# Decoder trunk on one core: the order of the block products in the FFNs, their weight sums, and a second plain channel pair

## The chip, the cores and the metric

The kernel runs on one core of a Trainium2 chip. The metric is the device time of one execution in microseconds. TensorE (PE in the profile) multiplies, VectorE (DVE), ScalarE (ACT) and GpSimd (POOL) do the rest, and SyncE (SP) issues most of the loads. Each engine takes its instructions in the order in which they were queued.

## The reference

Two layers over 512 tokens of 1024 channels, float32. Around each mixer (a gated DeltaNet in layer 0, spatial gating in layer 1) stand two half-step SwiGLU FFNs, four in all, with a norm before and after each part:

```python
def swiglu(h, w_gate, w_up, w_down):
    return (jax.nn.silu(h @ w_gate) * (h @ w_up)) @ w_down
...
x = x + 0.5 * rmsnorm(swiglu(rmsnorm(x, ng[0]), w_gate, w_up, w_down), ng[1])
```

The FFN is 2816 wide: `w_gate` and `w_up` are 1024 x 2816, `w_down` is 2816 x 1024. The change is in the FFNs alone.

## The kernel before

**Numbers.** Every float32 operand is kept as a high and a low part. `split` makes them: ScalarE casts the high part (L108), VectorE subtracts it from the source for the low part (L110). A product is then three matmuls: high by high, high by low, low by high.

**An FFN.** The 2816 channels are worked through in 11 pairs of 128 (`fp`, 256 channels). For each pair the gate and the up projection are computed, and `m` is their product after the SiLU. Then `proj_out` multiplies all of `m` with `w_down` (L332), into eight PSUM banks `y`, two for each of four token blocks.

**The first pair** is plain (`ffn_first`): for each half of the tokens, gate and up, two times 128 channels, eight blocks of depth and three matmuls of 128x128 by 128x256, 192 matmuls in all.

**The other ten pairs** take seven block products instead of eight (`seven`, once for gate and once for up: a group). The 256 channels, the 1024 deep and the 512 tokens are halved; sums of blocks of the weights and of the activations are made beforehand, and a group is seven products of 12 matmuls each (L393), into three of the eight banks: `pa`, `pb`, `pc`. Bank `pa` takes four products one on top of the other; after the first three of them `keep` (L401) saves what it holds so far by a ScalarE copy, before the next product adds to it. The products, by the names that the change gives them: p1 (weights `a11`, bank pa, then keep), p5 (`s1`, pc), p6 (`s2`, pa, then keep), p2 (`a12`, pb), p7 (`s3`, pa, then keep), p4 (`a22`, pa), p3 (`s4`, pc). After p2, p7, p4 and p3 a `sink` (`gate` or `up`) adds a kept copy to a bank (L477, L486), applies the SiLU (L479, L481) or multiplies into `m` (L488, L490).

`seven` is a generator; `ffn` advances a group and the one before it (`late`) in turns, which gives the order p1, p4 of the group before, p5, p3 of the group before, p6, p2, p7.

**Weights.** A planner queue holds all loads in the order of their use, each with a cost (1 for a plain half-depth tile, 3 for a group); `wget` takes the next and loads ahead until the cost of what is ready is 3. `wload_seven` prepares a group: two loads on SP's queue (L161) into tiles `raw`, of which there are four; the sums `su` (tile `wsum`): `su[:, 0]` and `su[:, 2]` on GpSimd (L165, L166), `su[:, 1]` and `su[:, 3]` on VectorE (L170, L174); and the splits into `wa` (a11, a12), `ws` (s1 to s4, two tiles) and `wd` (a22). All of these and the activations share 21 slots of one pool. Plain tiles are loaded by `wload` (L114) and split into `w`.

**Order.** The start of the kernel (the first loads, norms and splits) is written by hand; the rest of each engine's queue is put in order by a list scheduler, at compile time, from the program's order and a cost model.

Of the kernel before, what the change touches and what calls it, by code (L numbers as in the profile page):

```python
# [7 lines left out]
F32 = mybir.dt.float32  # L8
# [3 lines left out]
ALU = mybir.AluOpType  # L12
# [4 lines left out]
P = 128  # L17
S = 512
D = 1024
NT = S // P  # L20
KT = D // P
F = 2816
NF = F // P
# [4 lines left out]
class Trunk:  # L28
# [126 lines left out]
    def wload_seven(self, w, c0, part, spot):  # L155

        nc = self.nc
        raw = []
        for j in range(2):
            r = self.wp.tile([P, 4, 256], F32, tag="raw", name=self.nm("raw"))  # L160
            nc.sync.dma_start(out=r, in_=w[j * 512:(j + 1) * 512, c0:c0 + 256].rearrange("(k p) f -> p k f", p=P))  # L161
            raw.append(r)
        a = [[raw[j][:, :, i * P:(i + 1) * P] for j in range(2)] for i in range(2)]
        su = self.big([P, 4, 4, P], F32, name="wsum")
        nc.gpsimd.tensor_tensor(out=su[:, 0], in0=a[1][0], in1=a[1][1], op=ALU.add)  # L165
        nc.gpsimd.tensor_tensor(out=su[:, 2], in0=a[0][0], in1=a[1][0], op=ALU.subtract)  # L166
        w1 = self.big([P, 2, 2, 4, P], F32R, name="wa")
        for j in range(2):
            self.split(a[0][j], w1[:, 0, j], w1[:, 1, j])
        nc.vector.tensor_tensor(out=su[:, 1], in0=su[:, 0], in1=a[0][0], op=ALU.subtract)  # L170
        sums = []
        for n in range(2):
            if n:
                nc.vector.tensor_tensor(out=su[:, 3], in0=a[0][1], in1=su[:, 1], op=ALU.subtract)  # L174
            ws = self.big([P, 2, 2, 4, P], F32R, name="ws")
            self.split(su[:, 2 * n:2 * n + 2], ws[:, 0], ws[:, 1])
            sums += [(ws[:, 0, i], ws[:, 1, i]) for i in range(2)]
        if part == 0:
            spot.append(self.big([P, 2, 2, 4, P], F32R, name="wd"))
        w22 = spot[0][:, part]  # L180
        self.split(a[1][1], w22[:, 0], w22[:, 1])
        return {"a11": (w1[:, 0, 0], w1[:, 1, 0]), "a12": (w1[:, 0, 1], w1[:, 1, 1]),
                "s1": sums[0], "s2": sums[1], "s3": sums[2], "s4": sums[3], "a22": (w22[:, 0], w22[:, 1])}
# [136 lines left out]
            nc.sync.dma_start(out=store[:, c], in_=xo[:, c])  # L320


    def proj_out(self, get, nk, ntail, on_token, groups=(range(NT),), ready=None, need=None):

        need = need or (lambda kt: None)
        y = [[self.bank("y") for _ in range(2)] for _ in range(NT)]

        def step(kt, t, wt, hfs=(0, 1)):
            m = get(kt, t)
            for a, b in ((0, 0), (0, 1), (1, 0)):  # L330
                for hf in hfs:
                    self.nc.tensor.matmul(y[t][hf], m[a], wt[b][:, hf * 512:(hf + 1) * 512],  # L332
                                          start=(kt == 0 and a == 0 and b == 0),
                                          stop=(kt == nk - 1 and a == 1))

        nhead = nk - ntail
        tail = None
        for n, group in enumerate(groups):
            if n == 0:
                head = []  # L340
                for kt in range(nhead):
                    if kt == max(0, nhead - 10):
                        on_token.prepare()
                    need(kt)
                    wt, = self.wget()
                    if len(groups) > 1:
                        head.append(wt)
                    for t in group:
                        step(kt, t, wt)
                    self.tick()  # L350
                need(nk - 1)
                tail = self.wget(ntail)
            else:
                if n == 1:
                    self.drain_until(ready)
                for kt in range(nhead):
                    for t in group:
                        step(kt, t, head[kt])
                    self.tick()
            for t in group:  # L360
                last = t == NT - 1
                for i, kt in enumerate(range(nhead, nk)):
                    step(kt, t, tail[i], (0,) if last else (0, 1))
                    if i == 1 and len(groups) == 1:
                        self.tick()
                if last:
                    for i, kt in enumerate(range(nhead, nk)):
                        step(kt, t, tail[i], (1,))
                on_token(t, y[t][0], y[t][1])
                self.tick()  # L370
# [11 lines left out]
        return (slice(0, 256), slice(256, 512)) if first else (slice(0, S),)  # L382


    def seven(self, wts, a, sink):

        nc = self.nc
        ba, bb, bc = (self.bank("p" + n)[:, :256] for n in "abc")

        def prod(out, w, t, first, last):  # L390
            for k in range(4):
                for m, (x, y) in enumerate(((0, 0), (0, 1), (1, 0))):
                    nc.tensor.matmul(out, wts[w][x][:, k], t[y][:, k], start=(first and k == 0 and m == 0),  # L393
                                     stop=(k == 3 and m == 2), skip_group_check=not first)
            self.unit += 1
            if self.unit % 2 == 0:
                self.tick()

        def keep():
            s = self.tp.tile([P, 256], F32, tag="keep", name=self.nm("keep"), bufs=4)  # L400
            nc.scalar.copy(out=s, in_=ba)  # L401
            return s

        prod(ba, "a11", self.block(a, 0, 0), True, True)
        u1 = keep()
        yield
        prod(bc, "s1", self.tsum(a, 0), True, True)
        yield
        prod(ba, "s2", self.tsum(a, 1), False, True)
        u2 = keep()  # L410
        prod(bb, "a12", self.block(a, 1, 0), True, True)
        sink(0, 0, bb, u1)
        prod(ba, "s3", self.tsum(a, 2), False, True)
        u3 = keep()
        sink(1, 1, bc, u3)
        yield
        prod(ba, "a22", self.tsum(a, 3), False, True)
        sink(1, 0, ba, None)
        yield
        prod(bc, "s4", self.block(a, 1, 1), False, True)  # L420
        sink(0, 1, bc, u2)


    def plan_ffn(self, wg, wu, wd):
        self.plan_pair(wg, 0)
        self.plan_pair(wu, 0)
        for fp in range(1, NF // 2):
            spot = []
            self.plan_seven(wg, fp * 256, 0, spot)
            self.plan_seven(wu, fp * 256, 1, spot)  # L430
        self.plan_out(wd, NF, 5)
# [22 lines left out]
            nc.scalar.activation(out=sg, in_=pg[f], func=AF.Silu)  # L454
            nc.vector.tensor_tensor(out=m[:, f], in0=sg, in1=pu[f], op=ALU.mult)

    def ffn(self, a, on_token):
        nc = self.nc
        V = nc.vector
        self.unit = 0  # L460
        ms = []
        late = None
        for fp in range(NF // 2):
            if fp % 2 == 0:
                m4 = self.big([P, 4, S], F32, name="m")
            m = m4[:, fp % 2 * 2:fp % 2 * 2 + 2]
            ms.append(m)
            if fp == 0:
                self.ffn_first(a, m)
                continue  # L470
            sg = [self.half([P, S], name="sg") for _ in range(2)]
# [17 lines left out]
                elif i == 1:  # L489
                    V.tensor_tensor(out=m[:, 1, c], in0=sg[1][:, c], in1=ps if add is None else us[1][:, c], op=ALU.mult)  # L490

            for sink in (gate, up):
                wts, = self.wget()
                steps = self.seven(wts, a, sink)
                next(steps)
                if late:
                    next(late)
                next(steps)
                if late:
                    next(late, None)  # L500
                next(steps)
                late = steps
        for _ in late:
            pass
        split = {}

        def need(kt):
# [6 lines left out]
            b = split[kt // 2]  # L514
            return (b[:, 0, kt % 2, t * P:(t + 1) * P], b[:, 1, kt % 2, t * P:(t + 1) * P])

        self.proj_out(get, NF, 5, on_token, need=need)


class DeltaNet:  # L520
# [737 lines left out]
def trunk_kernel(ctx: ExitStack, tc: tile.TileContext, x, norm_g, ffn_w_gate, ffn_w_up, ffn_w_down,  # L1258
                 dn_w_in, dn_conv_w, dn_a_log, dn_dt_bias, dn_norm_g, dn_w_out, sg_w_in, sg_b_in,
                 sg_ln_g, sg_ln_b, sg_w_s, sg_b_s, sg_w_out, out):  # L1260
    K = Trunk(ctx, tc)
    nc = tc.nc
# [5 lines left out]
    st = St()  # L1268
# [54 lines left out]
    ffns = [[(ffn_w_gate[l, i], ffn_w_up[l, i], ffn_w_down[l, i]) for i in range(2)] for l in range(2)]  # L1323
    dn = DeltaNet(K, dn_w_in[0], dn_conv_w[0], dn_a_log[0], dn_dt_bias[0], dn_norm_g[0], dn_w_out[0])
    sg = SpatialGate(K, sg_w_in[0], sg_b_in[0], sg_ln_g[0], sg_ln_b[0], sg_w_s[0], sg_b_s[0], sg_w_out[0])
    K.plan_ffn(*ffns[0][0])
    dn.plan()
    K.plan_ffn(*ffns[0][1])
    K.plan_ffn(*ffns[1][0])
# [6 lines left out]
    def start(t):  # L1336
        w = K.big([P, D], F32, name="bt")
        gen = K.pre_norm(st.x[t // 2][:, t % 2], g0[:, 0], st.a, t, w, 1)
        next(gen)
        return gen  # L1340
# [5 lines left out]
    with tc.manual_schedule(engines={ET.SP, ET.Activation, ET.DVE, ET.Pool}):  # L1346
# [3 lines left out]
        first = [start(0), start(1)]  # L1350
# [9 lines left out]
        rest = [start(2), start(3)]  # L1360
# [2 lines left out]
    for t in range(2, NT):  # L1363
        K.tasks.append([K.clock + t, rest[t - 2]])

    K.ffn(st.a, boundary(1, 0.5, False, quad=False))
    with tc.issue_after(started[0]), tc.issue_after(started[1]):
        K.spawn(dn.consts())
    dn.run(st.a, boundary(3, 1.0, False))
# [29 lines left out]
```

## Time and profile before

| | |
|---|---|
| median of 3 runs | 2089.93 us (2089.32 to 2090.73) |
| profiled execution | 2089.82 us, span 2088.1 us |
| PE busy | 2018.2 us (97%) |
| DVE busy | 1346.7 us (64%) |
| ACT busy | 923.0 us (44%) |
| POOL busy | 378.9 us (18%) |
| instructions | 32220 |

Matmuls are pipelined, one begins before the one ahead has ended, and their ends are modelled; where TensorE works without a break the distance between two starts is the cost of one. Idle time of an engine counts only where something behind it is late. L12 is line 12 of the kernel before; many lines are helpers', so work is told apart by its tile.

### The profile page before, as it was taken

What the parts mean: (1) busy time and instruction counts of PE and PEld (TensorE: products, weight loads), DVE (VectorE), ACT (ScalarE), POOL (GpSimd) and SP (SyncE); (2) the same over time, 40 slices, a digit from 0 to 9 for tenths busy, and PEclk for the clock granted to TensorE, in tenths of its full rate; (3) what the DMA queues carried; (4) which work ended last, traced back from release to release, by engine and by line L of the source; (5) the groups of instructions that cost most, each with busy time, mean ns of one, the idle gap of its engine ahead of it and who ended that gap; (6) DMA issues with size and microseconds to landing.
All of it is one profiled execution on the core that took longest, in us unless ns stands there. A gap on an engine that the chain in (4) does not pass through costs nothing.

```text
span 2088.1 us, 32220 instructions
## 1 busy us (share of the span) xinstructions
PE 2018.2 (97%) x13182; PEld 1833.0 (88%) x13182; DVE 1346.7 (64%) x1803; ACT 923.0 (44%) x1640; POOL 378.9 (18%) x358
## 2 busy tenths in 40 slices
PE   7999999999999999999999999999999999999998
PEld 6999988888888899998889999888888889999887
DVE  5888652677846687875358887526465529777632
ACT  5554441585434554544245454424223426454521
POOL 3333100111142232320023222001000013232000
PEclk9999999999999999999999999999999999999999
DMA  4333352235221433336322333633322613333421
GB/s 143 102 103 100 112 203 72 91 102 151 92 77 62 142 91 101 101 102 212 101 71 81 102 104 99 217 101 110 107 87 87 223 50 103 101 94 99 172 91 41
DMA packets 159622, 229.63 MB, mean 110 GB/s; under 512 B 18745, under 2 KB 130673, under 8 KB 157042
## 3 DMA queue, kind: packets, MB, share of 16 engines
q1 hardware_dynamic: 150146, 195.90, 30.3%
q10 hardware_dynamic: 9328, 31.68, 3.9%
q8 instruction: 103, 1.69, 0.3%
q14 instruction: 45, 0.37, 0.1%
HBM read 213.34 MB, written 14.21 MB: 109 GB/s over the span
## 4 chain that ended last, share of the span: by engine, by line
PE 75%; DVE 14%; ACT 5%; issue 3%; POOL 2%; DMA 1%; ACTq 0%; DVEq 0%; POOLq 0%; SPq 0%
PE y L332 28%; PE pa L393 14%; PE pc L393 7%; PE pb L393 3%; DVE ws L110 2%; DVE wsum L170 2%; PE ph L198 2%; PE ph L200 2%; PE ph L199 2%; DVE wa L110 2%; ACT ws L108 1%; PE pv L198 1%; PE pu L198 1%; PE pv L199 1%; PE pu L199 1%
## 5 line engine op out<-in xcount | busy, mean ns | idle before, releaser
L332 PE MATMUL y<-w,ms 128*128 128x512 f32 x1632 | 370.7, 389 | 0.0
L332 PEld LDWEIGHTS y<-w,ms 128*128 128x128 f32 x1632 | 306.1, 188 | 63.3
L393 PE MATMUL pa<-hsh,ws 128*128 128x256 f32 x1280 | 259.9, 286 | 26.4 <-ACT keep L401 26.4
L110 DVE TENSOR_TENSOR w<-raw,w 128x1024 fp32r<-128x1024 f32 x162 | 195.8, 1223 | 68.9 <-ACT w L108 68.4
L393 PEld LDWEIGHTS pa<-hsh,ws 128*128 128x128 f32 x1280 | 211.5, 192 | 31.2 <-ACT keep L401 31.1
L108 ACT CAST ws<-wsum 128x1024 fp32r<-128x1024 f32 x160 | 166.9, 1050 | 161.5 <-DVE wsum L170 93.3
L165 POOL TENSOR_TENSOR wsum<-raw,raw 128x512 f32<-128x512 f32 x80 | 126.9, 1586 | 576.9 <-PE pb L393 124.9
L110 DVE TENSOR_TENSOR ws<-wsum,ws 128x1024 fp32r<-128x1024 f32 x160 | 206.5, 1302 | 17.8 <-ACT ws L108 17.7
L108 ACT CAST w<-raw 128x1024 fp32r<-128x1024 f32 x163 | 167.2, 1051 | 102.7 <-PE y L332 49.4
L393 PE MATMUL pa<-hsl,ws 128*128 128x256 f32 x640 | 181.5, 284 | 0.0
L310 DVE TENSOR_TENSOR bt<-y,gain 128x512 f32<-128x512 f32 x48 | 32.9, 688 | 180.4 <-ACT junk L306 179.5
L401 ACT COPY keep<-pa 128x256 f32<-128x256 f32 x240 | 88.2, 367 | 124.1 <-PE pa L393 124.1
L393 PE MATMUL pa<-hsh,wd 128*128 128x256 f32 x640 | 129.9, 286 | 13.2 <-ACT keep L401 13.2
L206 POOL TENSOR_TENSOR rstd<-ss 128x1 f32<-128x1 f32 x24 | 8.0, 331 | 740.2 <-ACT junk L306 740.2
L166 POOL TENSOR_TENSOR wsum<-raw 128x512 f32<-128x512 f32 x80 | 132.0, 1650 | 0.1
L393 PE MATMUL pa<-hq,wa 128*128 128x256 f32 x960 | 128.7, 284 | 0.0
L393 PE MATMUL pc<-hsh,ws 128*128 128x256 f32 x640 | 128.2, 283 | 0.0
L393 PE MATMUL pc<-hq,ws 128*128 128x256 f32 x960 | 128.2, 283 | 0.0
L393 PE MATMUL pb<-hq,wa 128*128 128x256 f32 x960 | 128.1, 283 | 0.0
L393 PEld LDWEIGHTS pa<-hsl,ws 128*128 128x128 f32 x640 | 123.1, 192 | 0.0
L393 PEld LDWEIGHTS pa<-hq,wa 128*128 128x128 f32 x960 | 121.5, 193 | 0.0
L393 PEld LDWEIGHTS pb<-hq,wa 128*128 128x128 f32 x960 | 121.0, 192 | 0.0
(300 smaller groups left out, 4356.6 us busy)
## 6 DMA issues: line engine op xcount, KB each, us to landing
raw<-in_ffn_w_gate SPq DMA_DIRECT2D x88, 512.0 KB, 3.7
raw<-in_ffn_w_up SPq DMA_DIRECT2D x88, 512.0 KB, 4.5
raw<-in_ffn_w_down SPq DMA_DIRECT2D x88, 512.0 KB, 4.3
raw<-in_dn_w_in SPq DMA_DIRECT2D x32, 512.0 KB, 4.4
raw<-in_sg_w_in SPq DMA_DIRECT2D x32, 512.0 KB, 3.8
xs<-x ACTq DMA_DIRECT2D x20, 512.0 KB, 2.6
x<-xs ACTq DMA_DIRECT2D x10, 1024.0 KB, 10.8
raw<-in_sg_w_out SPq DMA_DIRECT2D x16, 512.0 KB, 4.3
```

What stands on the lines that cost most here:

```text
L108: self.nc.scalar.copy(out=hi, in_=src)
L110: e.tensor_tensor(out=lo, in0=src, in1=hi.bitcast(F32), op=ALU.subtract)
L165: nc.gpsimd.tensor_tensor(out=su[:, 0], in0=a[1][0], in1=a[1][1], op=ALU.add)
L166: nc.gpsimd.tensor_tensor(out=su[:, 2], in0=a[0][0], in1=a[1][0], op=ALU.subtract)
L170: nc.vector.tensor_tensor(out=su[:, 1], in0=su[:, 0], in1=a[0][0], op=ALU.subtract)
L198: nc.tensor.matmul(out, lhsT[0], rhs[0], start=start, stop=False)
L199: nc.tensor.matmul(out, lhsT[0], rhs[1], start=False, stop=False)
L200: nc.tensor.matmul(out, lhsT[1], rhs[0], start=False, stop=stop)
L310: nc.vector.tensor_tensor(out=tmp[:, c], in0=y, in1=grow[:, c], op=ALU.mult)
L332: self.nc.tensor.matmul(y[t][hf], m[a], wt[b][:, hf * 512:(hf + 1) * 512], start=(kt == 0 and a == 0 and b == 0), stop=(kt == nk - 1 and a ...
L393: nc.tensor.matmul(out, wts[w][x][:, k], t[y][:, k], start=(first and k == 0 and m == 0), stop=(k == 3 and m == 2), skip_group_check=not f ...
L401: nc.scalar.copy(out=s, in_=ba)
```

## The change

Three edits, in all four FFNs unless said otherwise.

1. `wload_seven`: `su[:, 0]` and `su[:, 2]` are computed on VectorE, not on GpSimd, and in the text they stand behind the splits of a11 and a12.
2. `seven` returns the seven products as steps with places (0, 1, 3, 4, 6, 9, 12). Group number n begins at place 7n, so the order becomes p1, p5, p4 of the group before, p6, p2, p3 of the group before, p7. The two steps left after the last group (its p4 and p3) are run by `proj_out`, one ahead of each of its first two token steps. The weights are taken (`wget`) and the banks allocated in the step that first uses them.
3. In the first FFN alone the second channel pair is plain too (`plain=2`).

```diff
@@ wload_seven
-        nc.gpsimd.tensor_tensor(out=su[:, 0], in0=a[1][0], in1=a[1][1], op=ALU.add)
-        nc.gpsimd.tensor_tensor(out=su[:, 2], in0=a[0][0], in1=a[1][0], op=ALU.subtract)
         w1 = self.big([P, 2, 2, 4, P], F32R, name="wa")
         for j in range(2):
             self.split(a[0][j], w1[:, 0, j], w1[:, 1, j])
-        nc.vector.tensor_tensor(out=su[:, 1], in0=su[:, 0], in1=a[0][0], op=ALU.subtract)
+        V = nc.vector
+        V.tensor_tensor(out=su[:, 0], in0=a[1][0], in1=a[1][1], op=ALU.add)
+        V.tensor_tensor(out=su[:, 1], in0=su[:, 0], in1=a[0][0], op=ALU.subtract)
         sums = []
         for n in range(2):
             if n:
-                nc.vector.tensor_tensor(out=su[:, 3], in0=a[0][1], in1=su[:, 1], op=ALU.subtract)
+                V.tensor_tensor(out=su[:, 2], in0=a[0][0], in1=a[1][0], op=ALU.subtract)
+                V.tensor_tensor(out=su[:, 3], in0=a[0][1], in1=su[:, 1], op=ALU.subtract)
@@ proj_out
                     for t in group:
+                        if rest:
+                            rest.pop(0)()
                         step(kt, t, wt)
@@ seven
+        def p1():
+            nonlocal ba
+            wts.update(self.wget()[0])
+            ba = self.bank("pa")[:, :256]
+            prod(ba, "a11", self.block(a, 0, 0), True)
+            keep(1)
+
+        def p5():
+            nonlocal bc
+            bc = self.bank("pc")[:, :256]
+            prod(bc, "s1", self.tsum(a, 0), True)
+
+        def p6():
+            prod(ba, "s2", self.tsum(a, 1), False)
+            keep(2)
+
+        def p2():
+            nonlocal bb
+            bb = self.bank("pb")[:, :256]
+            prod(bb, "a12", self.block(a, 1, 0), True)
+            sink(0, 0, bb, kept[1])
+
+        def p7():
+            prod(ba, "s3", self.tsum(a, 2), False)
+            keep(3)
+            sink(1, 1, bc, kept[3])
+
+        def p4():
+            prod(ba, "a22", self.tsum(a, 3), False)
+            sink(1, 0, ba, None)
+
+        def p3():
+            prod(bc, "s4", self.block(a, 1, 1), False)
+            sink(0, 1, bc, kept[2])
+
+        return {0: p1, 1: p5, 3: p6, 4: p2, 6: p7, 9: p4, 12: p3}
@@ plan_ffn
-        self.plan_pair(wg, 0)
-        self.plan_pair(wu, 0)
-        for fp in range(1, NF // 2):
+        for fp in range(plain):
+            self.plan_pair(wg, fp * 256)
+            self.plan_pair(wu, fp * 256)
+        for fp in range(plain, NF // 2):
@@ ffn
-            if fp == 0:
+            if fp < plain:
                 self.ffn_first(a, m)
                 continue
...
-            for sink in (gate, up):
-                wts, = self.wget()
-                steps = self.seven(wts, a, sink)
-                next(steps)
-                if late:
-                    next(late)
-                next(steps)
-                if late:
-                    next(late, None)
-                next(steps)
-                late = steps
-        for _ in late:
-            pass
+            for n, sink in enumerate((gate, up)):
+                first = (2 * (fp - plain) + n) * 7
+                for place, step in self.seven(a, sink).items():
+                    places[first + place] = step
+                for place in range(first, first + 7):
+                    if place in places:
+                        places.pop(place)()
+        rest = [places.pop(place) for place in sorted(places)]
...
-        self.proj_out(get, NF, 5, on_token, need=need)
+        self.proj_out(get, NF, 5, on_token, need=need, rest=rest)
@@ trunk_kernel
-    K.plan_ffn(*ffns[0][0])
+    K.plan_ffn(*ffns[0][0], plain=2)
...
-    K.ffn(st.a, boundary(1, 0.5, False, quad=False))
+    K.ffn(st.a, boundary(1, 0.5, False, quad=False), plain=2)
```

## Rows read from the trace of the kernel before

**Rows 1.** Page, part 1: engine, busy us, share of the span, instructions.

```profile
PE 2018.2 (97%) x13182; PEld 1833.0 (88%) x13182; DVE 1346.7 (64%) x1803; ACT 923.0 (44%) x1640; POOL 378.9 (18%) x358
```

**Rows 2.** Waits: engine, line, waited for, total us, times, longest us.

```profile
ACT ws L108 <- DVE wsum L170: 93.3, 55, 5.7
...
POOL wsum L165 <- DMA raw<-in_ffn_w_up: 59.0, 7, 11.2
...
PE pa L393 <- ACT keep L401: 39.6, 39, 2.1
```

**Rows 3.** Timeline of PE, 188 to 192 us: start, length, work, idle before.

```profile
188.36 0.28 PE L393 MATMUL pa<-hsh,ws 128*128 128x256 f32 x1
188.48 1.60 PE L393 MATMUL pa<-hq,wa 128*128 128x256 f32 x12
191.68 0.39 PE L393 MATMUL pa<-hsh,wd 128*128 128x256 f32 x1 [1.61 <-ACT keep L401]
191.91 0.28 PE L393 MATMUL pa<-hsl,wd 128*128 128x256 f32 x1
```

**Rows 4.** Timeline of ACT, 190 to 194 us.

```profile
190.31 1.04 ACT L108 CAST ws<-wsum 128x1024 fp32r<-128x1024 f32 x1 [4.08 <-DVE wsum L170]
191.27 0.37 ACT L401 COPY keep<-pa 128x256 f32<-128x256 f32 x1
...
193.32 0.36 ACT L401 COPY keep<-pa 128x256 f32<-128x256 f32 x1
```

**Rows 5.** Windows: stretch, busy us by engine, granted clock, DMA share, GB/s.

```profile
168.00:189.00 21.00, 21.00 (x178) 21.00 (x177) 14.19 (x19) 7.62 (x15) 5.58 (x4) 1.00 0.26 76
189.00:210.00 21.00, 18.41 (x152) 18.00 (x151) 20.02 (x26) 11.85 (x21) 6.10 (x4) 1.00 0.35 102
```

**Rows 6.** Groups of instructions: busy us, mean ns, idle before, releasers.

```profile
L110 DVE TENSOR_TENSOR ws<-wsum,ws 128x1024 fp32r<-128x1024 f32 x160 | 206.5, 1302 | 17.8 <-ACT ws L108 17.7
...
L165 POOL TENSOR_TENSOR wsum<-raw,raw 128x512 f32<-128x512 f32 x80 | 126.9, 1586 | 576.9 <-PE pb L393 124.9 <-DVE ws L110 116.9 <-PE pc L393 104.7
...
L170 DVE TENSOR_TENSOR wsum<-wsum,raw 128x512 f32<-128x512 f32 x80 | 84.1, 1052 | 13.9 <-POOL wsum L165 13.9
L110 DVE TENSOR_TENSOR wd<-raw,wd 128x512 fp32r<-128x512 f32 x80 | 83.3, 1054 | 2.8 <-ACT wd L108 2.8
...
L174 DVE TENSOR_TENSOR wsum<-raw,wsum 128x512 f32<-128x512 f32 x80 | 69.5, 869 | 1.1
```

**Rows 7.** Timeline of DVE, 110 to 116 us.

```profile
110.23 1.28 DVE L110 TENSOR_TENSOR wa<-raw,wa 128x512 fp32r<-128x512 f32 x2
111.44 0.68 DVE L170 TENSOR_TENSOR wsum<-wsum,raw 128x512 f32<-128x512 f32 x1
...
113.57 1.21 DVE L110 TENSOR_TENSOR ws<-wsum,ws 128x1024 fp32r<-128x1024 f32 x1
115.97 1.77 DVE L170 TENSOR_TENSOR wsum<-wsum,raw 128x512 f32<-128x512 f32 x1 [1.19 <-POOL wsum L165]
```

**Rows 8.** Timeline of POOL, 106 to 118 us.

```profile
115.90 1.29 POOL L166 TENSOR_TENSOR wsum<-raw 128x512 f32<-128x512 f32 x1
```

**Rows 9.** Timeline of ACT, 24 to 38 us.

```profile
31.44 1.05 ACT L108 CAST ws<-wsum 128x1024 fp32r<-128x1024 f32 x1 [5.75 <-DVE wsum L170]
...
35.85 2.04 ACT L108 CAST hq<-pt 128x512 fp32r<-128x512 f32 x4
```

**Rows 10.** Timeline of PE, 29 to 73 us.

```profile
29.33 1.04 PE L265 MATMUL pt<-ident,bt 128*128 128x128 f32 x8
...
32.95 0.28 PE L200 MATMUL pu<-hq,w 128*128 128x256 f32 x1
37.46 0.57 PE L198 MATMUL pg<-hq,w 128*128 128x256 f32 x2 [4.23 <-ACT hq L108]
...
71.90 1.60 PE L393 MATMUL pa<-hq,wa 128*128 128x256 f32 x12
```

**Rows 11.** Windows at the start of the second token half, columns as in rows 5.

```profile
39.00:45.00 6.00, 5.87 (x29) 5.87 (x30) 4.81 (x8) 2.15 (x3) 0.67 (x1) 0.54 0.23 77
```

More of the change, by code (lines that the diff above doesn't have):

```diff
@@ L320, in post_norm, with proj_out @@
             nc.sync.dma_start(out=store[:, c], in_=xo[:, c])
-    def proj_out(self, get, nk, ntail, on_token, groups=(range(NT),), ready=None, need=None):
+    def proj_out(self, get, nk, ntail, on_token, groups=(range(NT),), ready=None, need=None, rest=()):
         need = need or (lambda kt: None)
+        rest = list(rest)
         y = [[self.bank("y") for _ in range(2)] for _ in range(NT)]
@@ L382, in halves, with seven, prod @@
         return (slice(0, 256), slice(256, 512)) if first else (slice(0, S),)
-    def seven(self, wts, a, sink):
+    def seven(self, a, sink):
         nc = self.nc
-        ba, bb, bc = (self.bank("p" + n)[:, :256] for n in "abc")
-        def prod(out, w, t, first, last):
+        wts = {}
+        ba, bb, bc = None, None, None
+        kept = {}
+        def prod(out, w, t, first):
             for k in range(4):
@@ L397, in prod, with keep, plan_ffn @@
                 self.tick()
[L399 to L424, printed above, removed]
-        self.plan_pair(wg, 0)
-        self.plan_pair(wu, 0)
-        for fp in range(1, NF // 2):
+        def keep(n):
+            kept[n] = self.tp.tile([P, 256], F32, tag="keep", name=self.nm("keep"), bufs=4)
+            nc.scalar.copy(out=kept[n], in_=ba)
+        def p1():
[27 more added lines that the diff above has]
+        return {0: p1, 1: p5, 3: p6, 4: p2, 6: p7, 9: p4, 12: p3}
+    def plan_ffn(self, wg, wu, wd, plain=1):
+        for fp in range(plain):
+            self.plan_pair(wg, fp * 256)
+            self.plan_pair(wu, fp * 256)
+        for fp in range(plain, NF // 2):
             spot = []
@@ L455, in ffn_first, with ffn @@
             nc.vector.tensor_tensor(out=m[:, f], in0=sg, in1=pu[f], op=ALU.mult)
-    def ffn(self, a, on_token):
+    def ffn(self, a, on_token, plain=1):
         nc = self.nc
@@ L461, in ffn @@
         ms = []
-        late = None
+        places = {}
         for fp in range(NF // 2):
```

## The prediction

> **What bounds the kernel now.** I read the page first. TensorE is busy 2018.2 of 2088.1 us [rows 1], so all that any change can remove, short of matmuls, is about 70 us of idle TensorE. Who owns it is in the view of waits: one pair alone, a matmul into bank pa that waits for ScalarE's copy `keep`, accounts for 39.6 us in 39 stops [rows 2]. The reader is to see what it waits for: no weight, but the copy that saves bank pa before the next product accumulates into it.
>
> Then one stop, on TensorE's timeline. Twelve matmuls of a product take (1.60 - 0.28) / 11 = 0.12 us each, 1.44 us a product [rows 3]. At 188.48 p1 of a group is issued; p4 of the group before is next and could begin at 189.92, but begins at 191.68 and its second matmul comes 0.23 us after the first [rows 3]. The stop is shown as 1.61 us; it loses 191.68 - 189.92 + 0.11 = 1.87 us, so I add 0.26 to 0.27 to each stop shown. With that, the 39 stops lose 39.6 + 39 x 0.27 = 50.1 us. ScalarE's timeline says why: the copy ends at 191.64, behind a cast of weight sums that had waited 4.08 us for VectorE's L170 [rows 4]. ScalarE works in order, so a copy that takes 0.37 us is late by whatever cast stands ahead of it. VectorE is the late one: it is busy 20.02 of the 21 us from 189 on, and 14.19 in the 21 us before, in which TensorE never stops [rows 5]. So VectorE is full in clusters, though 64% busy over all [rows 1].
>
> **The change part by part.**
>
> *Order of the products.* Before, a group g and the one before it (') ran p1, p4', p5, p3', p6, p2, p7. After: p1, p5, p4', p6, p2, p3', p7. What stands between a product and the next one on the same bank: after p6 two products instead of one (p2, p3'), after p7 two instead of one (p1, p5 of the next group), after p1 two instead of three. Every stop seen so far is after p6 or p7, so each gets 1.44 us more cover. Work on TensorE is the same.
>
> How much of the stops goes? In the first FFN they are, in us: 1.16, 0.30, 0.39, 1.21; 1.05, 1.23; 0.54; 1.61, 0.99; 2.06; 0.52. I grouped them by the clusters in which VectorE is full, because a cluster that is behind stays behind: cover is spent once in it, not once a stop. So a cluster gives back its whole loss, but 1.44 us at most. The last stop (0.52, and one like it in each FFN) stays, for p4 still follows p7 at once at the tail. That gives, without the first FFN's first cluster, 5.1, 7.5, 7.5 and 7.3 us in the four FFNs: 27.4 us. Bounds: if every stop but the tail's goes, 50.1 - 4 x 0.79 = 47.0 us.
>
> Against it stands p1. A copy after p7 that ended 3.00 us after the modelled end of its product (188.64 to 191.64) cost 1.87, so a copy is free up to 1.12 us with one product behind it and up to 2.56 with two [rows 3, 4]. The copy after p1 at 188.48 (modelled end 190.08) ends at 193.68, 3.60 us late; three products covered it, two would not [rows 3, 4]. Pairing every copy with its product, I find 17 of 80 after p1 over 2.56 us, by 12.8 us in all. Between 0 (their casts come sooner, see next) and 12.8 I take half, 6.4 us.
>
> The sinks move with the products: each remains one VectorE or ScalarE instruction of 0.4 to 0.7 us, its banks are released at most two products later, and eight banks hold three of one group and two of the last. Cost nil; cover gone, a bank would have to be late by more than a group. The two leftover steps go in front of the first two token steps of the down projection, whose last bank is needed after two more: nil too.
>
> *Sums on VectorE.* L165 and L166 ran on GpSimd, 1.59 us on average for L165, and each of 80 weight sets has both [rows 6]. On VectorE no such sum with su[:, 0] stands, but L170 has the same shape and operand kinds: 0.68 us alone, and two instructions of that size in a row take 1.28, so the second adds 0.60 [rows 7]. 160 more instructions are 96 us. What is taken away: L170 began at 115.97 while GpSimd's L166 ran 115.90 to 117.19, and took 1.77 instead of 0.68 [rows 7, 8]. Means over the kernel against their value alone: L170 1.052, L174 0.869 and wd 1.054 against 0.68, ws 1.302 against 1.21 [rows 6, 7]. That is 80 x (0.37 + 0.19 + 0.37) + 160 x 0.09 = 89 us of VectorE time which GpSimd's presence costs. So 96 in, 89 out: nil on VectorE, and the chain sum, cast, difference is shorter by a GpSimd step. Bounds: 0 to 96 us taken back.
>
> The Trainium skill, SBUF — State Buffer, "Who interferes with whom", says that a VectorE instruction with two SBUF inputs contends with a GpSimd instruction that reads SBUF, and that one of them blocks. The trace agrees: 1.77 us against 0.68 for the same sum. By that rule the sums on VectorE would be paid for by the end of this blocking, as in my sum.
>
> In order, a first sum that waits for its raw tile now holds up VectorE: the sinks, the differences and through their casts the copies. On GpSimd it waited for raw data 59.0 us in seven cases for `up` alone [rows 2], harmlessly. Bounds: nil, or GpSimd's mean idle before it, 576.9 / 80 = 7.2 us a set [rows 6]. In the new text it stands behind the two splits of the same tiles, which need the data too, so I take nil.
>
> *Second plain pair.* One pair costs TensorE 192 matmuls instead of 168: 24 x 0.12 = +2.88 us. It takes the first seven-product set out of the start. There ScalarE idled 5.75 us for L170 before the cast at 31.44, and the four casts of the second token half stood behind it until 35.85 [rows 9]; TensorE had finished the first half at 33.07 and began the second at 37.46, after a stop of 4.23 us; from 39 to 45 us its granted clock was 0.54, about the lower of its levels (1.2 against 2.4 GHz) [rows 10, 11]. Without that: 33.07 + 96 x 0.12 + 192 x 0.12 = 67.6 us, where the third group then begins. It begins at 71.90 now [rows 10]: 4.3 us gained, with the extra matmuls paid. If the casts stay as late, the pair instead costs 2.88 less the 2.0 us of its own stops, +0.9. The transposes of the last token block end at 30.37 [rows 10] and four casts and differences need some 2 us, so I take the gain. Its four loads on SP's queue are the same bytes, one at a time instead of two. The first cluster's other stops, 0.39 and 1.21 (2.1 us lost), should go, as two weight sets fewer are prepared up to there.
>
> Sum: 27.4 + 4.3 + 2.1 - 6.4 = 27.4 us off. The profiled execution took 2089.82 (span 2088.1), the runs' median is 2089.93, the same within 0.01%. 2089.8 - 27.4 = **2062 us**.
>
> **Rivals.**
>
> 1. *The cover is only moved.* p1's shorter cover costs the full 12.8 us or more, because with earlier stops gone the copies are later still against TensorE. For it: after 188.48, p7's and p1's copies stand behind the same casts [rows 4]. Against it: those casts wait for L170, which gets faster. 12.8 instead of 6.4, and half of the start's gain: about 2071.
>
> 2. *All stops go.* If the end of the blocking also empties the clusters: 47.0 + 4.3, of which 2.0 are counted twice: about 2041.
>
> 3. *VectorE pays in full (slower).* In the stretches where it is full, 20 of 21 us, VectorE can take nothing more [rows 5]. Two sets there bring 4 x 0.60 = 2.4 us; four such stretches an FFN, 16 in all, 39 us, and the cover is used up: 2062 + 39 = 2101. It decides when more than 27.4 / 16 = 1.7 us of a stretch isn't paid by the blocking that ends. Against it: 89 us of stretched instructions lie mostly in just these stretches. The Trainium skill, Perfetto Trace Analysis, "Optimizing Scalar/DVE Operations", says that work of a saturated VectorE may be offloaded, even to GpSimd, which speaks against this move; it adds that the shared port can spoil that. The rows side with the second half.
>
> 4. *No change.* The order of ScalarE's queue is made anew from the new program; where its copies land behind other casts the stops come back at other places, and only the start's few us remain: 2086 to 2092.
>
> **How the numbers follow.** My forecast 0.50, rival 1 0.21, rival 2 0.10, rival 3 0.09, rival 4 0.10. About 0.2% (4 us) is what a measurement here tells from no change. Faster: the first three, and little of the fourth, 0.82; same 0.09; slower 0.09. The range reaches from near rival 2 past rival 1 to the edge of rival 4: 2044 to 2084.
>
> **What would show it.** Right: the waits of pa for `keep` fall under 15 us, TensorE's busy time rises by 2 to 3 us only, L170, L174 and wd show means near 0.68 us, VectorE's busy time stays within 25 us, the third group's weights start near 67.6. Wrong: stops before p6 (after p1) of over 12 us; VectorE idle before the first sum; stretches with VectorE at 21 of 21 and TensorE waiting for `ws` or `wa`.

## The result and the profile after

The changed kernel takes 2036.82 us (median; 2033.23 to 2039.26) against 2089.62 for the one before: ratio 0.975, 95% interval 0.9726 to 0.9774. It is faster, as forecast, but by 52.8 us where 27.4 were forecast, and outside the range of 2044 to 2084.

Parts of the page of the changed kernel (busy time), its view of waits, its groups of instructions, three of its windows of 21 us (columns as in [rows 5]) and rows of TensorE's timeline follow; three points mark rows left out. Line numbers have moved: the copy `keep` is L408, the products L400, the four sums L169, L170, L174, L175.

```profile
PE 2012.0 (99%) x13206; PEld 1833.3 (90%) x13206; DVE 1324.3 (65%) x1942; ACT 920.6 (45%) x1627; POOL 122.2 (6%) x198
```

```profile
ACT keep L408 <- PE pa L400: 147.8, 121, 4.0
ACT ws L108 <- DVE wsum L170: 100.9, 71, 3.6
...
PE pa L400 <- ACT keep L408: 2.1, 4, 0.5
```

```profile
L110 DVE TENSOR_TENSOR ws<-wsum,ws 128x1024 fp32r<-128x1024 f32 x156 | 189.2, 1220 | 10.9 <-ACT ws L108 9.7
...
L170 DVE TENSOR_TENSOR wsum<-wsum,raw 128x512 f32<-128x512 f32 x78 | 53.2, 682 | 0.0
L169 DVE TENSOR_TENSOR wsum<-raw,raw 128x512 f32<-128x512 f32 x78 | 53.2, 682 | 0.0
...
L110 DVE TENSOR_TENSOR wd<-raw,wd 128x512 fp32r<-128x512 f32 x78 | 52.0, 684 | 2.7 <-ACT wd L108 2.7
```

```profile
89.00:110.00 21.00, 21.00 (x177) 21.00 (x176) 20.94 (x34) 13.31 (x23) 0.00 (x0) 1.00 0.41 126
110.00:131.00 21.00, 21.00 (x177) 21.00 (x176) 13.90 (x25) 8.78 (x16) 0.00 (x0) 1.00 0.26 76
131.00:152.00 21.00, 21.00 (x177) 21.00 (x176) 20.89 (x35) 12.27 (x23) 0.00 (x0) 1.00 0.45 132
```

```profile
34.93 0.38 PE L200 MATMUL pg<-hq,w 128*128 128x256 f32 x1 [0.74 <-DVE hq L110]
...
68.38 1.60 PE L400 MATMUL pa<-hq,wa 128*128 128x256 f32 x12
...
247.62 0.39 PE L400 MATMUL pa<-hsh,wd 128*128 128x256 f32 x1 [0.52 <-ACT keep L408]
...
249.27 1.09 PE L334 MATMUL y<-w,ms 128*128 128x512 f32 x4
```

The waits of `pa` for `keep` have gone from 39 to 4 [rows 2], one at the tail of each FFN, as the row at 247.62. VectorE's two-input instructions of the weight sets are back at their value alone: 0.68 us for the sums and `wd`, 1.22 for `ws`, where means of 1.05, 1.05 and 1.30 stood [rows 6]. VectorE is as full in its clusters as before, 20.94 of 21 us against 20.02 [rows 5], and TensorE runs through them without a gap. That last reading is the one to hold on to: the forecast took a full VectorE for the reason why the copies are late.

Where the time came from, by stage, each from its first product to its first token step (L334, before L332), with 1.44 us added after for the product p3 that now follows that step:

| us | before | after | difference |
|---|---|---|---|
| start of the kernel to the first FFN's token steps | 268.11 | 250.71 | -17.40 |
| second FFN | 213.96 | 202.48 | -11.48 |
| third FFN | 215.14 | 202.49 | -12.65 |
| fourth FFN | 213.39 | 202.49 | -10.90 |
| all between them | | | +1.8 |

The sum is -50.6 us, the difference of the two profiled spans (2088.1 and 2037.5). The +1.8 holds one more stretch of 6.8 us at the lower TensorE clock in the DeltaNet stage, and about 1.7 of the third FFN's gain is such a stretch, 3.4 us long, that only the trace of before has. Another, 6.8 us long from 37.6 us on [rows 11], is gone from the start of the kernel and is worth some 3 us there.

### The profile page after: what moved, and what is told of

It is laid out like the page before. It is cut to its first block, busy times and chain, and to the rows that moved or that the text cites. A ratio compares the mean times of both kernels' runs of the same rounds, so it can differ in the third digit from the quotient of the medians.

```text
span 2037.5 us, 32054 instructions
## 1 busy us (share of the span) xinstructions
PE 2012.0 (99%) x13206; PEld 1833.3 (90%) x13206; DVE 1324.3 (65%) x1942; ACT 920.6 (45%) x1627; POOL 122.2 (6%) x198
## 3 DMA queue, kind: packets, MB, share of 16 engines
q8 instruction: 103, 1.69, 0.3%
## 4 chain that ended last, share of the span: by engine, by line
PE 96%; DVE 1%; ACT 1%; issue 1%; POOL 0%; DMA 0%; ACTq 0%; DVEq 0%; SPq 0%; POOLq 0%
PE y L334 30%; PE pa L400 22%; PE pc L400 11%; PE pb L400 6%; PE pu L201 2%; PE pu L200 2%; PE pu L199 2%; PE ph L199 2%; PE ph L201 2%; PE ph L200 2%; PE pv L199 1%; PE pv L200 1%; PE pv L201 1%; PE pa L1075 1%; PE pg L200 1%; PE pg L201 1%
## 5 line engine op out<-in xcount | busy, mean ns | idle before, releaser
L334 PE MATMUL y<-w,ms 128*128 128x512 f32 x1632 | 372.5, 389 | 0.0
L334 PEld LDWEIGHTS y<-w,ms 128*128 128x128 f32 x1632 | 305.5, 188 | 63.2
L400 PE MATMUL pa<-hsh,ws 128*128 128x256 f32 x1248 | 250.1, 283 | 0.0
L110 DVE TENSOR_TENSOR w<-raw,w 128x1024 fp32r<-128x1024 f32 x166 | 200.4, 1222 | 71.0 <-ACT w L108 70.7
L108 ACT CAST ws<-wsum 128x1024 fp32r<-128x1024 f32 x156 | 161.7, 1051 | 118.0 <-DVE wsum L170 100.9
L108 ACT CAST w<-raw 128x1024 fp32r<-128x1024 f32 x167 | 170.8, 1051 | 97.2 <-DMA raw<-in_ffn_w_down 35.8
L400 PEld LDWEIGHTS pa<-hsh,ws 128*128 128x128 f32 x1248 | 205.9, 192 | 0.0
L110 DVE TENSOR_TENSOR ws<-wsum,ws 128x1024 fp32r<-128x1024 f32 x156 | 189.2, 1220 | 10.9 <-ACT ws L108 9.7
L400 PE MATMUL pa<-hsl,ws 128*128 128x256 f32 x624 | 176.6, 283 | 0.0
L408 ACT COPY keep<-pa 128x256 f32<-128x256 f32 x234 | 86.5, 370 | 150.2 <-PE pa L400 147.8
L400 PE MATMUL pa<-hsh,wd 128*128 128x256 f32 x624 | 125.4, 284 | 2.1 <-ACT keep L408 2.1
L400 PE MATMUL pc<-hq,ws 128*128 128x256 f32 x936 | 126.3, 283 | 0.0
L400 PE MATMUL pa<-hq,wa 128*128 128x256 f32 x936 | 125.4, 283 | 0.0
L400 PE MATMUL pc<-hsh,ws 128*128 128x256 f32 x624 | 125.0, 283 | 0.0
L400 PE MATMUL pb<-hq,wa 128*128 128x256 f32 x936 | 125.0, 283 | 0.0
L400 PEld LDWEIGHTS pa<-hsl,ws 128*128 128x128 f32 x624 | 119.8, 192 | 0.0
L307 ACT ACTIVATE junk<-y 128x512 bf16<-128x512 f32 x48 | 28.7, 597 | 201.5 <-PE y L334 200.7
L400 PEld LDWEIGHTS pc<-hq,ws 128*128 128x128 f32 x936 | 119.0, 192 | 0.7
L400 PEld LDWEIGHTS pa<-hq,wa 128*128 128x128 f32 x936 | 118.1, 192 | 0.0
L400 PEld LDWEIGHTS pb<-hq,wa 128*128 128x128 f32 x936 | 117.9, 192 | 0.0
L334 PE MATMUL y<-wtail,ms 128*128 128x512 f32 x480 | 111.0, 390 | 0.0
## 6 DMA issues: line engine op xcount, KB each, us to landing
x<-xs ACTq DMA_DIRECT2D x10, 1024.0 KB, 11.7
```

Of the source, the lines that this page charges most:

```text
L108: self.nc.scalar.copy(out=hi, in_=src)
L110: e.tensor_tensor(out=lo, in0=src, in1=hi.bitcast(F32), op=ALU.subtract)
L307: nc.scalar.activation(out=junk[:, :512], in_=y, func=AF.Square, scale=1.0 / (32.0 * gain), accum_out=s2[:, i:i + 1])
L408: nc.scalar.copy(out=kept[n], in_=ba)
```

## Experiments

The change has three parts, so each was first made alone. Theory A, that of the prediction: the order's longer cover removes the stops, the sums are nil. Theory B: the stops are made by GpSimd's reads, which stretch VectorE's instructions; without them the copies come in time under any order.

**Sums alone.** Order and plain pairs as before.

```diff
-        nc.gpsimd.tensor_tensor(out=su[:, 0], in0=a[1][0], in1=a[1][1], op=ALU.add)
-        nc.gpsimd.tensor_tensor(out=su[:, 2], in0=a[0][0], in1=a[1][0], op=ALU.subtract)
...
+        V.tensor_tensor(out=su[:, 0], in0=a[1][0], in1=a[1][1], op=ALU.add)
...
+                V.tensor_tensor(out=su[:, 2], in0=a[0][0], in1=a[1][0], op=ALU.subtract)
```

> The kernel before with the four weight sums on VectorE; the order of the products and the plain pair as before. Theory A (the second product of cover removed the stops, the sums are neutral): 2082 to 2090 us, some 39 stops for the copy keep. Theory B (the copies were late because the sums on GpSimd held up VectorE and through it the casts ahead of the copies): the copies come on time with one product of cover too, 2045 to 2055 us, the waits of pa for keep under 10 us.

Measured: 2038.39 us, ratio 0.9764 (0.9749 to 0.9778). From the page (busy time), the waits, and TensorE's timeline at the start:

```profile
PE 2007.8 (99%) x13182; PEld 1828.9 (90%) x13182; DVE 1333.0 (65%) x1963; ACT 925.6 (45%) x1640; POOL 122.2 (6%) x198
```

```profile
ACT keep L402 <- PE pa L394: 209.3, 126, 4.6
...
PE pa L394 <- ACT keep L402: 2.6, 5, 0.6
```

```profile
34.91 0.51 PE L199 MATMUL pg<-hq,w 128*128 128x256 f32 x2 [1.90 <-ACT hq L108]
36.70 0.39 PE L200 MATMUL pg<-hq,w 128*128 128x256 f32 x1 [1.05 <-DVE hq L110]
```

This part alone brings nearly all, more than either theory expected: 5 stops are left with the old order's single product of cover. The copies now wait for TensorE more than before, 126 times and 209.3 us; the row of the kernel before is this:

```profile
ACT keep L401 <- PE pa L393: 124.1, 99, 2.8
```

VectorE is busy 13.7 us less than before, though it executes 160 instructions more. The start gains too: 1.90 and 1.05 us of stops stand where 4.23 [rows 10] and then 0.68 stood.

**Order alone.** GpSimd keeps its sums.

```diff
-    def seven(self, wts, a, sink):
+    def seven(self, a, sink):
...
+        return {0: p1, 1: p5, 3: p6, 4: p2, 6: p7, 9: p4, 12: p3}
```

> The kernel before with the products interleaved seven steps apart; sums on GpSimd and one plain pair as before. Theory A: nearly all stops go, 2043 to 2050 us. Theory B: the copies remain up to 3.6 us late, so stops of up to 1 us remain after p1 and p6, 2062 to 2075 us. In both, L170 and wd keep means near 1.05 us.

Measured: 2068.09 us, ratio 0.991 (0.9892 to 0.9927). The waits, and one of the stops on TensorE's timeline:

```profile
PE pa L399 <- ACT keep L407: 19.4, 30, 1.0
```

```profile
191.66 0.39 PE L399 MATMUL pa<-hsh,ws 128*128 128x256 f32 x1 [0.96 <-ACT keep L407]
```

About 21 us, which is the prediction's 27.4 - 6.4 for this part, and 30 stops are left. Twelve of them, 7.75 us, stand before p6, as the one shown: there p1's copy is late, and before the change no stop stood there. On the whole the copies are not earlier under this order (after p1 and p7 they are later), they are only better covered. How late a copy ends after the modelled end of its product, with each copy on ScalarE's timeline paired to its product on TensorE's (mean and worst, us):

| copy after | before | order alone | sums alone | changed kernel |
|---|---|---|---|---|
| p1 | 1.47, 3.60 | 1.69, 3.79 | 0.60, 2.52 | 0.74, 1.47 |
| p6 | 1.10, 3.45 | 0.89, 3.44 | 0.56, 2.92 | 0.62, 1.76 |
| p7 | 0.81, 3.00 | 1.26, 3.85 | 0.46, 0.75 | 0.47, 0.98 |

**Both.** Sums and order, one plain pair: the diff of the change without its `plain=2`.

> The changed kernel with one plain pair in the first FFN instead of two. Both theories: no stops but the tails', and the start as before, the first FFN 6 to 9 us longer than in the changed kernel: 2043 to 2046 us.

Measured: 2038.33 us, ratio 0.9764 (0.9749 to 0.9779), below the range expected of both theories and the same as the sums alone; on top of them the order is worth nothing that shows.

**Second plain pair alone.**

```diff
-    K.plan_ffn(*ffns[0][0])
+    K.plan_ffn(*ffns[0][0], plain=2)
```

> The kernel before with the second plain pair in the first FFN alone. Both theories: the start gains 6 to 9 us (late casts of the second token half and the first cluster's stops), the other stops stay: 2081 to 2084 us. If the pair pays only together with the sums on VectorE: 2088 to 2091 us.

Measured: 2081.18 us, ratio 0.9965 (0.9954 to 0.9977), 8.0 us faster. Its stops are those of before but for the first FFN's first ones: 35 are left, with 35.8 us.

So B holds over A. But "without GpSimd's sums" is two things: nothing on GpSimd reads SBUF (theory C), and a step through another engine is gone from the chain sum, cast, copy (theory D). The next three runs part them.

**GpSimd reads, nobody waits for it.** The sums alone, and GpSimd does two additions of the same tiles into a scratch tile that nobody reads.

```diff
+        for x, y in ((a[1][0], a[1][1]), (a[0][0], a[1][0])):
+            idle = self.tp.tile([P, 4, P], BF16, tag="idle", name=self.nm("idle"), bufs=1)
+            nc.gpsimd.tensor_tensor(out=idle, in0=x, in1=y, op=ALU.add)
```

> The kernel with only the sums moved to VectorE, and GpSimd doing two additions of the same raw tiles for every weight set into a scratch tile (bfloat16) that nobody reads: GpSimd reads SBUF as before, but no sum waits for it. Theory C (what made the copies late was the stretching of VectorE's two-input instructions while GpSimd reads SBUF): stretched instructions and stops return, 2065 to 2090 us. Theory D (it was the step through GpSimd, 2.6 us and more, that L170 and the casts had to wait for): 2036 to 2044 us.

Measured: 2156.84 us, ratio 1.0334 (1.0318 to 1.0349), 118 us over the sums alone and far above the range expected of either theory. The waits, the groups, and one stop on four timelines:

```profile
ACT ws L108 <- DVE wsum L173: 169.9, 76, 9.7
PE pa L397 <- ACT keep L405: 74.7, 44, 4.2
```

```profile
L172 DVE TENSOR_TENSOR wsum<-raw,raw 128x512 f32<-128x512 f32 x80 | 85.4, 1067 | 0.0
...
L177 DVE TENSOR_TENSOR wsum<-raw 128x512 f32<-128x512 f32 x80 | 68.8, 860 | 0.0
```

```profile
127.11 1.76 POOL L171 TENSOR_TENSOR idle<-raw,raw 128x512 bf16<-128x512 f32 x1 [2.95 <-DMA raw<-in_ffn_w_up]
128.94 1.63 POOL L171 TENSOR_TENSOR idle<-raw 128x512 bf16<-128x512 f32 x1
```

```profile
127.63 1.78 DVE L177 TENSOR_TENSOR wsum<-raw 128x512 f32<-128x512 f32 x1
129.34 0.41 DVE L490 TENSOR_TENSOR us<-pc,keep 128x256 f32<-128x256 f32 x1
129.67 1.45 DVE L173 TENSOR_TENSOR wsum<-wsum,raw 128x512 f32<-128x512 f32 x1
```

```profile
131.15 1.04 ACT L108 CAST ws<-wsum 128x1024 fp32r<-128x1024 f32 x1 [4.04 <-DVE wsum L173]
132.41 1.04 ACT L108 CAST ws<-wsum 128x1024 fp32r<-128x1024 f32 x1 [0.21 <-DVE wsum L178]
133.36 0.61 ACT L108 CAST wd<-raw 128x512 fp32r<-128x512 f32 x1
133.88 0.36 ACT L405 COPY keep<-pa 128x256 f32<-128x256 f32 x1
```

```profile
134.30 0.58 PE L397 MATMUL pa<-hsh,wd 128*128 128x256 f32 x1 [3.28 <-ACT keep L405]
```

This is the whole mechanism in one place. While GpSimd adds, from 127.11 on, VectorE's L177 takes 1.78 us and L173 1.45, each 0.68 alone. L490 between them, with one operand from a PSUM bank, keeps its 0.41. ScalarE's cast waits 4.04 us for L173; two more casts stand ahead of the copy in ScalarE's queue; the copy ends at 134.24 and TensorE has stood 3.28 us. The queues of TensorE and ScalarE hold the same instructions in the same order as with the sums alone, and VectorE's too but for one sum, at 740 us, that stands two places earlier; no load waits for the additions. So the durations make the difference. Over the whole execution 142 of VectorE's 128x512 instructions with two SBUF inputs overlap an addition by more than 0.3 us: they take 1.32 us on average and 1.82 at most. The other 418 take at most 0.69.

The two profiled spans differ by 122 us (2158.3 and 2036.3). The stops shown are 74.7 of it, and with 0.27 for each restart 87, of which the sums alone have 4 as well. Most of the rest is TensorE's lower clock. After the stop shown the granted clock is 0.72 on the mean from 134 to 140 us: 3.4 us at the lower level, then the higher again. Over the whole execution it is 0.981, against 0.996 for the sums alone, from which I estimate the loss at 2158.3 x 0.019 - 2036.3 x 0.004 = 33 us. Together that is 116 of the 122 us.

**A step through GpSimd that reads nothing.** The sums alone, with a memset of the sums' tile by GpSimd ahead of the first sum.

```diff
+        nc.gpsimd.memset(su[:, 0:3], 0.0)
```

> The kernel with only the sums moved to VectorE, and a GpSimd memset of three quarters of the sum tile ahead of the first sum of every weight set: the step through GpSimd is back, but GpSimd reads nothing. Theory C: no instruction is stretched, 2036 to 2044 us. Theory D: the sums come late again behind GpSimd, ACT waits for L170 as before, 2060 to 2085 us.

Measured: 2040.32 us, ratio 0.9777 (0.9763 to 0.9792). The groups, and one memset beside two of VectorE's sums (of another set):

```profile
L169 POOL MEMSET wsum<- 128x1536 f32 x80 | 110.6, 1382 | 683.3 <-PE pa L395 180.3 <-PE pb L395 165.7 <-DVE ws L110 144.1
...
L170 DVE TENSOR_TENSOR wsum<-raw,raw 128x512 f32<-128x512 f32 x80 | 54.6, 682 | 0.3 <-POOL wsum L169 0.3
```

```profile
132.44 1.38 POOL L169 MEMSET wsum<- 128x1536 f32 x1 [9.46 <-PE pa L395]
```

```profile
132.60 0.69 DVE L175 TENSOR_TENSOR wsum<-raw 128x512 f32<-128x512 f32 x1
133.21 0.69 DVE L171 TENSOR_TENSOR wsum<-wsum,raw 128x512 f32<-128x512 f32 x1
```

GpSimd is busy 110 us more, VectorE's sums stay at 0.68 us and the time stays. In all 77 of VectorE's 128x512 instructions with two SBUF inputs overlap a memset by more than 0.3 us, and none takes over 0.69. The Trainium skill, SBUF — State Buffer, "Who interferes with whom", says that a VectorE instruction with two SBUF inputs contends with a GpSimd instruction that reads SBUF, not with one that only writes it; these two runs show both halves (0.69 at most beside a memset, up to 1.82 beside an addition). As a test of D it is weak: the memset needs no weights and was done before VectorE came to the sums, which waited for it 0.3 us in all. So D isn't refuted in general; C is enough by itself, as the run before shows. In the kernel before, VectorE waited 13.9 us in all for GpSimd's sums [rows 6], against the 89 us by which its instructions were stretched.

**Half of the sums.** The first sum on VectorE, `su[:, 2]` left on GpSimd.

```diff
-        nc.gpsimd.tensor_tensor(out=su[:, 0], in0=a[1][0], in1=a[1][1], op=ALU.add)
+        V.tensor_tensor(out=su[:, 0], in0=a[1][0], in1=a[1][1], op=ALU.add)
```

> The kernel before with one of the two GpSimd sums moved, su[:, 0], which L170 needs; su[:, 2] stays on GpSimd. Theory C: half of the reading stays, so about half of the stops, 2052 to 2070 us. Theory D: the first cast no longer waits for GpSimd, 2036 to 2046 us.

Measured: 2067.11 us, ratio 0.9906 (0.9889 to 0.9922). 30 stops:

```profile
PE pa L394 <- ACT keep L402: 21.6, 30, 1.2
```

Half of GpSimd's reads gone, 21 of the 51 us gained, as C would have it. The first pair of sums has no GpSimd step any more here, and TensorE still stops 30 times; the second pair has one still, so by itself this run doesn't shut out D.

**The same additions on VectorE.** The scratch additions of above, `nc.gpsimd` replaced by `V`: the load that rival 3 feared.

```diff
-            nc.gpsimd.tensor_tensor(out=idle, in0=x, in1=y, op=ALU.add)
+            V.tensor_tensor(out=idle, in0=x, in1=y, op=ALU.add)
```

> The kernel with only the sums moved, and the same two additions into a scratch tile that GpSimd did in e_busy now done by VectorE: some 100 us more work for VectorE, none of it stretched, and none for GpSimd. If e_busy was slow because VectorE had about 100 us more to do: 2130 to 2157 us. If stretching at moments that the queue order does not foresee is what makes the copies late: 2036 to 2060 us. Rival 3's count, an added 2.4 us in each of some 16 full stretches, would be about 2077 us.

Measured: 2039.99 us, ratio 0.9778 (0.976 to 0.9796), as fast as the sums alone within what can be told. Its page, and its windows:

```profile
PE 2007.7 (99%) x13182; PEld 1828.6 (90%) x13182; DVE 1424.6 (70%) x2123; ACT 926.1 (45%) x1640; POOL 124.4 (6%) x198
```

```profile
100.00:121.00 21.00, 21.00 (x177) 21.00 (x176) 21.00 (x37) 11.11 (x21) 0.00 (x0) 1.00 0.34 101
121.00:142.00 21.00, 21.00 (x177) 21.00 (x176) 19.07 (x32) 10.75 (x20) 0.00 (x0) 1.00 0.33 102
142.00:163.00 21.00, 21.00 (x177) 21.00 (x176) 20.96 (x35) 12.50 (x22) 0.00 (x0) 1.00 0.37 103
163.00:184.00 21.00, 21.00 (x177) 21.00 (x176) 19.01 (x32) 10.50 (x20) 0.00 (x0) 1.00 0.32 101
```

And the first two of these windows with the additions on GpSimd:

```profile
100.00:121.00 21.00, 18.73 (x154) 18.33 (x153) 21.00 (x32) 11.50 (x20) 4.41 (x3) 1.00 0.35 104
121.00:142.00 21.00, 17.72 (x135) 17.52 (x134) 15.88 (x20) 7.46 (x15) 8.32 (x6) 0.92 0.34 98
```

VectorE is busy 1424.6 us here, 92 more than with the sums alone, and 1452.9 with the additions on GpSimd, nearly the same load; the times are 117 us apart. Here VectorE is busy 80.0 of the 84 us shown and TensorE never waits in them. A VectorE full of planned work is not what stops TensorE, and rival 3 falls with it.

**Sums and the second plain pair, old order.**

> The changed kernel without the new order of the products: sums on VectorE and the second plain pair alone. If the order adds nothing once the copies are on time: 2035 to 2039 us, as the changed kernel.

Measured: 2036.42 us, ratio 0.9756 (0.974 to 0.9772), the changed kernel's time without its new order. Its edit is the first and fourth diffs of this section together.

**The tail stop, twice.** Four stops of 0.52 us are left in the changed kernel, where p4 follows p7 at once. First the leftover steps one token later:

```diff
-                        if rest:
+                        if rest and t:
```

> The changed kernel with the two leftover steps of each FFN one token step later in the down projection, so that one step stands between p7 and p4: the four stops of 0.52 us go, each with some 0.27 us behind it: 3.2 us less than the changed kernel, 2033 to 2035 us, unless the last bank of y now waits for pc.

Measured: 2033.06 us, ratio 0.9742 (0.9727 to 0.9757). The number fell where it was expected, but not by the edit: the stop still stands at 247.59, p4 still follows p7, only p3 moved, and the FFN's stages have the changed kernel's lengths. Its 3.8 us lie within the changed kernel's own spread. The second try ties the steps behind the first token step on TensorE:

```diff
-                        if rest:
-                            rest.pop(0)()
+                        if rest and t:
+                            with self.tc.issue_after(self.ystep.ins):
+                                rest.pop(0)()
```

> As e_tail, but with the leftover steps held behind the first token step of the down projection on TensorE's queue, since in e_tail p4 was queued straight behind p7 again. The four stops of 0.52 us go: 3 us less than the changed kernel, 2031 to 2035 us; if the first token step's own inputs are late, no gain.

Measured: 2040.59 us, ratio 0.9771 (0.9756 to 0.9787). TensorE's timeline:

```profile
248.68 2.14 PE L334 MATMUL y<-w,ms 128*128 128x512 f32 x8 [1.46 <-ACT ms L108]
```

The 0.52 is gone and 1.46 stands in its place: the token step now comes before its cast `ms`. No gain was to be had there, and no version beat the changed kernel by more than its spread.

## Why the prediction was half right

**What bounds the kernel: right.** The stops of `pa` for `keep` were the prize, and the restart of 0.27 us on top of each as well. 39.6 us of stops fell to 2.1. TensorE's busy time fell by 6.2 us instead of rising by 2 to 3: the restarts are counted as busy, and 2.88 - 35 x 0.27 = -6.6. That sign was overlooked.

**"VectorE is the late one", "cover is spent once in a cluster": the step that failed.** The prediction saw L170 at 1.77 us [rows 7, 8], priced it, and then used it only as a sum: 96 us in, 89 out, nil. The sum held within 14 us (VectorE's busy time went from 1346.7 to 1333.0 with the sums alone). But it is the wrong quantity. What stopped TensorE was that single instructions took 1.1 us longer at moments at which a cast, and behind it a copy, stood waiting in a queue whose order is fixed; a full VectorE with its instructions at their usual length does no harm (the same additions on VectorE, on GpSimd: 2039.99 and 2156.84). Having booked the sums at nil, the prediction took the copies' lateness as given and left the whole gain to the cover. The term of the sum for the stops, 5.1 + 7.5 + 7.5 + 7.3 + 2.1 - 6.4 = 23.1 us, came out at 11.0 + 11.5 + 12.7 + 10.9 = 46.1 (11.0 is the first FFN without its start, below), close to the prediction's bound of 47.0, at which every stop but the tails' goes.

**Order of the products: the sum came out, in part by luck, and it didn't count.** Alone it brings the 21 us worked out, but neither term is right. The stops before p6, behind p1's copy, cost 7.75 + 12 x 0.27 = 11.0 us, where 6.4 were taken. Those before p7 and p4 fell from 50.1 us to 11.7 + 18 x 0.27 = 16.5, so 33.6 us came back, where 27.4 were counted by the rule of one cover a cluster. The two errors nearly cancel. With the sums moved there is nothing left to cover: sums alone, sums and order, and sums and second pair stand at 0.9764, 0.9764 and 0.9756. The price at p1 was not paid in the changed kernel, where no copy after p1 is over 1.47 us late.

**Second plain pair: short by 2.1 us.** The third group's weights were to start at 67.6 us and did at 68.38, as the second token half still stops for 0.74. But the old start was misread: at 71.90 [rows 10] the leftover p4 and p3 of the set before were still to come, 2.88 us, so the gain is 71.90 + 2.88 - 68.38 = 6.4 us, not 4.3. Either part alone brings most of it. With the second plain pair alone the first weights of a group start at 68.51. With the sums alone the second token half starts at 34.91 instead of 37.46, and the third group's weights at 66.19 with 2.88 us of work still to come. So the two don't add up: on top of the sums the pair is worth 2 us, which is within the spread (2038.39 and 2036.42).

**The rivals.** Rival 2, "all stops go", is what happened, by the condition it named, the end of the blocking; its 2041 is 4 us high, 2 of them the start. It had 0.10 because the end of the blocking was credited only with busy time. Rival 3's condition, that VectorE isn't paid back, didn't arise, and 92 us of planned load more on VectorE cost nothing that shows. 1424.6 us of work on VectorE are harmless in this kernel, and two additions a weight set on GpSimd cost 117 us. The Trainium skill, Perfetto Trace Analysis, "Optimizing Scalar/DVE Operations", allows moving work of a saturated VectorE to GpSimd, and says that the port which they share may undo the gain. This kernel shows the second. Rivals 1 and 4 fell with the stops, though rival 1 named the price of p1 better: the order alone shows 11.0 of its 12.8 us.

**What stays open.** Why ScalarE's queue takes 92 us more planned VectorE work without a stop, and not the stretched instructions: the order is laid out from planned durations, so that more work shifts the places and a stretch doesn't. The orders fit this: against the sums alone, ScalarE's queue is the same with the additions on GpSimd and differs at 235 of 1640 places with them on VectorE. It wasn't tried by itself. Moving the sums also gave ScalarE a new order (359 places differ from before); whether the order of before, without stretched instructions, would still have stops wasn't tried either.

## What to carry to other kernels

An instruction stretched by another engine is priced by when it falls and by who stands behind it in the fixed queues, not by the change in busy time: follow one stop from TensorE through the late copy and cast to the one instruction that took too long, and ask what made it long. A full engine on the way isn't yet a cause; give it a planned load of the same size and see whether the stops come. Undo the parts one at a time: alone they gained 51, 21 and 8 us, together 53.

## What the hardware did that was not expected

160 additions on GpSimd that nobody waits for, some 262 us of GpSimd's time, made a kernel 118 us slower: VectorE's 128x512 sums took up to 1.82 instead of 0.68 us, and stops of TensorE, with stretches at its lower clock behind them, followed. GpSimd's additions take 1.64 us on average there (262.4 / 160), the shortest 1.28.
